# A causal convolution moved whole onto TensorE, in eight phases, two channel tiles side by side

## The chip, the cores and the metric

The program runs on one core of a Trainium2 chip. The metric is device time in microseconds (us) of one launch; the kernel before takes 1869.24 us, the median of three runs (1868.62 to 1869.81).

## The reference, cut to what matters

The whole model is two blocks (mixer, cross attention, MLP, then a conformer convolution, feed-forward, banded attention, feed-forward) on 512 tokens of width 1024 in float32. The change is in the convolution alone:

```python
def conformer_conv(x, w_pw1, b_pw1, w_dw, b_dw, ln_g, ln_b, w_pw2, b_pw2):
    a = jax.nn.glu(x @ w_pw1 + b_pw1, axis=-1)          # 1024 -> 2 x 1024, gated
    y = lax.conv_general_dilated(a, w_dw[:, None, :], window_strides=(1,),
        padding=((CONV_WIDTH - 1, 0),), feature_group_count=D_MODEL) + b_dw   # 31 taps, each channel for itself
    y = jax.nn.silu(layernorm(y, ln_g, ln_b))           # mean and variance over the 1024 channels of a token
    return y @ w_pw2 + b_pw2
```

Each channel has its own 31 taps over the last 31 tokens. LayerNorm needs all 1024 channels of a token before the first product with w_pw2.

## The kernel before, in words

Activations lie with channels on the 128 partitions: eight tiles t = 0 to 7 of 128 channels, 512 tokens along the free axis. A product in float32 precision is made of three fp32r matmuls (high by high, low by high, high by low, lines 396 to 398), so one output tile of a 1024-wide product takes 24 matmuls of 512 columns. Weights come by DMA as units of 512 KB (`raw`, on the queue of SyncE), and ScalarE and VectorE split each into `wH` and `wL`.

The convolution stage, `ph_con`, goes over the tiles: for tile t TensorE makes the value half `pa` and the gate half `pg`; `open_gates(t - 1)` makes the gated tile on VectorE and ScalarE. Then the taps. Two tiles (DIRECT) are done on VectorE: `chains` is a generator of 31 multiply-adds per tile, and `fill(n)` slips n of them between other work. Six tiles (PHASED) go to TensorE: the gated tile is written with its tokens sorted by token number modulo 4, and `to_phases` sends it to DRAM (`ph0x` to `ph7x`) and reads it back so that a partition is (phase, 32 channels). A convolution is then nine matmuls with small weight matrices for each group of 32 channels, whose output has tokens on the partitions; `phased(t)` makes 4 groups x 9 matrices. The matrices come from DRAM in loads of 16 (1 MB, tile `mat`, on the queue of GpSimd) into the pool `a8` of eight buffers; four of these hold the input x until the last pointwise matmul has read it, so that four or eight loads can be there at a time. A load waits until the matmuls have read the load whose buffer it takes.

A float32 matmul appears in the trace as two records, one for each half of the weights; an fp32r matmul and a transpose appear as one.

`take(t)` adds the bias and puts the result into `Y` (tokens on partitions, channels along the free axis), `bn_stats` makes sums over it, and after the last tile `bn_aggr` joins them, `newton` makes the reciprocal root, `normalise` applies it on `Y`, `turn` transposes back on TensorE, and `gate` applies SiLU and splits the result for the product with w_pw2. `keep_warm` (line 473) issues matmuls of no use while TensorE would wait.

The stage lies within `tc.manual_schedule()`: what order the code is written in is the order on each engine; DMAs of the SyncE queue are issued in their order, and each issue waits for what it needs before the next can go. The taps of the last tile (`phased(last, ...)`) stand behind those of tiles 5 and 6 and the transposes of the DIRECT tiles. In the chain and timeline rows `pc` is the bank that taps write, `xp` a tile read back in phases, `mat` the weight matrices, `glu` a gated tile, `ct` the transposes, `cz` and `ycH` the SiLU and its high part. In the banded attention, later in the program, `bo` is the product of weights with values: line 1771 writes it by halves of 64 columns of the array, j = 0 and 1 in turn.

Of the kernel before, what the change touches and what calls it, by code (L numbers as in the profile page):

```python
# [53 lines left out]


DIRECT, PHASED = [0, 1], [2, 3, 4, 5, 6, 7]

CHAIN = (6, 6, 6, 10, 10, 10, 10, 8)

NMAT = 9  # L60
# [7 lines left out]
WARM = (13, 22, 5)  # L68
# [28 lines left out]
def shape_constants():  # L97
# [8 lines left out]
    for h in range(8):  # L106
# [5 lines left out]
    return np.concatenate([ident, ones, causal, glam, reset, sel, oh, neg], axis=1)  # L112
# [3 lines left out]
      "reset": (512, 512), "sel": (1024, 8), "oh": (1032, 384), "neg": (1416, 384)}  # L116
# [113 lines left out]
def matrix_order():  # L230

    return [(t, g, m) for t in PHASED for g in range(4) for m in range(NMAT)]


def pack_matrices(inp):


    w = np.asarray(inp["conv_w_dw_2"])[0]
    order = matrix_order()
    out = np.zeros((-(-len(order) // 16), P, 16, P), np.float32)  # L240
    for n, key in enumerate(order):
        a = out[n // 16, :, n % 16, :]
        t, g, m = key
        c = np.arange(32)
        for s in range(4):
            for r in range(4):
                k = 4 * m + s - r - 2
                if 0 <= k < TAPS:
                    a[32 * s + c, 32 * r + c] = w[k, t * P + 32 * g + c]
    return out  # L250
# [21 lines left out]
class Builder:  # L272
# [1116 lines left out]
    def ph_con(self, ph):  # L1389
        nc, tc = self.nc, self.tc  # L1390
        x = self.x
        with tc.tile_pool(name="pc", bufs=1) as pool:

            Y = pool.tile([P, 4, D], F32, name="cY")
            bdw = pool.tile([P, D], F32, name="cb")
            stat = pool.tile([P, 4, (NT + 1) * 6], F32, name="cst6")
            nc.sync.dma_start(out=bdw, in_=bass.AP(self.row.tensor, self.row.offset, [[0, P], [1, D]]))
            wd = lambda t, k: self.col("w_dw", t * TAPS + k)
            gates, glus, xs, banks, mats, done = {}, {}, {}, {}, [], {}
            place = {key: n for n, key in enumerate(matrix_order())}  # L1400
            W_ = 4 * (P + NMAT - 1)
# [13 lines left out]
            def padded(name):  # L1415
                return pool.tile([P, W_], F32, tag="glu", name=self.nm(name), bufs=6)


            def to_phases(t):
                d = self.dp.tile([P, W_], F32, name=f"ph{t}x")  # L1420
                nc.sync.dma_start(out=d, in_=glus[t])
                xp = xs[t] = padded("xp").rearrange("p (g q) -> p g q", g=4)
                q = W_ // 4
                for s in range(4):
# [3 lines left out]
            def phased(t, gs=range(4)):  # L1428

                ps = banks[t] = self.bank("pc")  # L1430
                for g in gs:
# [5 lines left out]
            def chains():  # L1437
                for t in DIRECT:
                    while t not in glus:
                        yield  # L1440
                    acc = [pool.tile([P, S], F32, tag="cy", name=self.nm("cy"), bufs=3) for _ in range(2)]
                    for k in range(TAPS):
                        a, tap = acc[k % 2], glus[t][:, 2 + k:2 + k + S]
                        if k < 2:
                            nc.vector.tensor_scalar(a, tap, wd(t, k), None, ALU.mult)
                        else:
                            nc.vector.scalar_tensor_tensor(a, tap, wd(t, k), a, ALU.mult, ALU.add)
                        yield
# [369 lines left out]
```

## Time and profile before

| what | us |
|---|---|
| median of three runs | 1869.24 |
| the profiled execution, its own time | 1869.69 |
| its span in the trace | 1867.9 |
| TensorE busy (9177 matmul records) | 1845.1 (99%) |
| weight loads of TensorE, beside matmuls | 1515.9 (81%) |
| VectorE busy | 974.4 (52%) |
| ScalarE busy | 692.8 (37%) |
| GpSimd busy | 240.5 (13%) |
| DMA queue of SyncE, share of 16 engines | 27.8% |
| DMA queue of GpSimd, share of 16 engines | 3.6% |

The chain of work that ended last lies on TensorE for 88% of the span, and the granted clock of TensorE is 0.997 over the span. The taps on TensorE (line 1433) are 3% of that chain. Times in the rows below are microseconds from the start of the span.

### The profile page before, as it was taken

The page shows a single profiled execution, that of the slowest core. Times are in us where ns is not written, and L with a number is a line of the kernel's source. Part 1 is how long each engine was busy: PE and PEld are TensorE (multiplying, and loading weights), DVE is VectorE, ACT ScalarE, POOL GpSimd, SP SyncE. Part 2 cuts the span into 40 slices and gives each one's busy share as a digit, 9 for nine tenths or more (in the row PEclk, how much of TensorE's full clock was granted, in tenths as well). Part 3 has the DMA queues.
Part 4 walks back from the last instruction along what each step waited for, and adds up shares of the span by engine and source line. Part 5 has one row for each costly group of instructions (what it writes and reads, how often), then busy time and mean ns, then how long its engine had stood idle before and what let it go on. Part 6 is the DMA issues. An engine that isn't in the chain of part 4 may idle for free.

```text
span 1867.9 us, 23231 instructions
## 1 busy us (share of the span) xinstructions
PE 1845.1 (99%) x9177; PEld 1515.9 (81%) x9177; DVE 974.4 (52%) x1690; ACT 692.8 (37%) x1136; POOL 240.5 (13%) x237
## 2 busy tenths in 40 slices
PE   9999999999999999999999999999999999999997
PEld 6877778888888888889788888888877888888886
DVE  6658755765343444586654434245677444343444
ACT  5546654543232324311233223133566432132232
POOL 0111001020000000200022001011354211010110
PEclk9999999999999999999999999999999999999998
DMA  5313222122332323456132332654221232323321
GB/s 188 104 58 128 87 90 91 58 90 92 101 100 92 101 91 101 168 172 223 62 113 97 103 102 84 119 146 138 91 68 35 79 95 97 101 88 96 101 90 55
DMA packets 60653, 191.32 MB, mean 102 GB/s; under 512 B 6352, under 2 KB 16592, under 8 KB 58752
## 3 DMA queue, kind: packets, MB, share of 16 engines
q1 hardware_dynamic: 55152, 169.04, 27.8%
q0 software_dynamic: 2720, 17.83, 3.6%
q10 hardware_dynamic: 2672, 2.97, 0.5%
q8 instruction: 72, 1.18, 0.3%
q14 instruction: 37, 0.30, 0.1%
HBM read 182.90 MB, written 6.91 MB: 102 GB/s over the span
## 4 chain that ended last, share of the span: by engine, by line
PE 88%; issue 4%; DVE 4%; ACT 2%; DMA 1%; POOL 1%; SPq 0%; POOLq 0%; ACTq 0%; DVEq 0%
PE mm L396 26%; PE mm L397 26%; PE mm L398 26%; PE pc L1433 3%; DMA raw<-in_w_dram 1%; DVE wL L375 1%; PE bo L1771 1%; DVE q L1679 1%; PE fs L880 1%; PE ft L895 1%; PE fo L908 1%; ACT wH L374 1%; PE ps L506 0%; PE bs L1728 0%; PE bt L1754 0%
## 5 line engine op out<-in xcount | busy, mean ns | idle before, releaser
L374 ACT CAST wH<-raw 128x1024 fp32r<-128x1024 f32 (+1 forms) x304 | 315.5, 1041 | 881.6 <-PE mm L397 623.2
L396 PE MATMUL mm<-xH,wH 128*128 128x512 f32 x1232 | 481.5, 391 | 0.9 <-ACT wH L356 0.6
L397 PE MATMUL mm<-xL,wH 128*128 128x512 f32 x1232 | 479.7, 389 | 1.0 <-DVE xL L537 1.0
L398 PE MATMUL mm<-xH,wL 128*128 128x512 f32 x1232 | 479.6, 389 | 0.0
L375 DVE TENSOR_TENSOR wL<-raw,wH 128x1024 fp32r<-128x1024 f32 (+1 forms) x304 | 371.3, 1222 | 114.6 <-ACT wH L374 106.0
L396 PEld LDWEIGHTS mm<-xH,wH 128*128 128x128 f32 x1232 | 231.3, 188 | 50.8 <-issue 1.7
L397 PEld LDWEIGHTS mm<-xL,wH 128*128 128x128 f32 x1232 | 231.3, 188 | 48.7 <-DVE xL L537 1.3
L398 PEld LDWEIGHTS mm<-xH,wL 128*128 128x128 f32 x1232 | 231.3, 188 | 48.3 <-DVE wL L357 0.2
L396 PE MATMUL mm<-hidH,wH 128*128 128x512 f32 (+1 forms) x615 | 237.9, 387 | 0.0
L397 PE MATMUL mm<-hidL,wH 128*128 128x512 f32 (+1 forms) x615 | 237.8, 387 | 0.0
L398 PE MATMUL mm<-hidH,wL 128*128 128x512 f32 (+1 forms) x615 | 237.7, 387 | 0.0
L550 DVE TENSOR_TENSOR h<-mm,h 128x512 f32<-128x512 f32 x103 | 71.1, 691 | 263.7 <-PE mm L398 263.7
L499 POOL TENSOR_TENSOR ssq<-ssq,sq 128x512 f32<-128x512 f32 (+1 forms) x49 | 78.3, 1598 | 626.3 <-ACT sq L498 619.6
L1372 POOL TENSOR_TENSOR g<-g,rbc 128x512 f32<-128x512 f32 x44 | 75.1, 1708 | 538.3 <-ACT g L1371 538.3
L396 PEld LDWEIGHTS mm<-hidH,wH 128*128 128x128 f32 x615 | 115.5, 188 | 24.1 <-issue 0.6
L397 PEld LDWEIGHTS mm<-hidL,wH 128*128 128x128 f32 x615 | 115.5, 188 | 23.4
L398 PEld LDWEIGHTS mm<-hidH,wL 128*128 128x128 f32 x615 | 115.5, 188 | 23.4
L1373 DVE TENSOR_TENSOR g<-mm,g 128x512 f32<-128x512 f32 x44 | 30.1, 691 | 124.0 <-PE mm L398 119.4
L1370 DVE TENSOR_TENSOR g<-mm,rbc 128x512 f32<-128x512 f32 x44 | 30.2, 691 | 100.5 <-PE mm L398 98.5
L1339 DVE SCALAR_TENSOR_TENSOR u<-mm,rbc 128x512 f32<-128x512 f32 x32 | 21.9, 691 | 76.9 <-PE mm L398 75.8
L396 PE MATMUL mm<-wH,xH 128*128 128x512 f32 (+1 forms) x160 | 60.2, 376 | 0.0
L398 PE MATMUL mm<-wH,xL 128*128 128x512 f32 (+1 forms) x160 | 59.0, 369 | 0.0
(326 smaller groups left out, 2344.1 us busy)
## 6 DMA issues: line engine op xcount, KB each, us to landing
raw<-in_w_dram SPq DMA_DIRECT2D x272, 512.0 KB, 3.5
mat<-in_mat_dram POOLq DMA_DIRECT2D x14, 1024.0 KB, 7.5
raw<-in_w_dram SPq DMA_DIRECT2D x32, 448.0 KB, 3.2
rel<-rt POOLq DMA_DIRECT2D x1, 3072.0 KB, 35.6
h<-in_x_dram SPq DMA_DIRECT2D x8, 256.0 KB, 5.3
raw<-in_w_dram SPq DMA_DIRECT2D x8, 256.0 KB, 5.5
bias<-rel SPq DMA_DIRECT2D x1, 2048.0 KB, 8.9
mem<-in_mem_dram ACTq DMA_DIRECT2D x4, 256.0 KB, 3.7
```

The costliest lines, as they stand in the source:

```text
L374: self.nc.scalar.copy(H[:, :n], raw[:, :n])
L375: self.low = lambda: self.nc.vector.tensor_tensor(L[:, :n], raw[:, :n], H[:, :n].bitcast(F32), ALU.subtract)
L396: mm(out, lhsT=aH, rhs=bH, start=start, stop=False)
L397: mm(out, lhsT=aH, rhs=bL, start=False, stop=False)
L398: mm(out, lhsT=aL, rhs=bH, start=False, stop=stop)
L499: (eng or nc.gpsimd).tensor_tensor(self.ssq[:, :n], self.ssq[:, :n], q[:, :n], ALU.add)
L550: nc.vector.tensor_tensor(self.h[:, t, :], ps, self.h[:, t, :], ALU.add)
L1339: nc.vector.scalar_tensor_tensor(t, ps, 0.0, rb, ALU.max, ALU.mult)
L1370: nc.vector.tensor_tensor(g, pg, rb, ALU.mult)
L1372: nc.gpsimd.tensor_tensor(g, g, rb, ALU.mult)
L1373: nc.vector.tensor_tensor(g, pu, g, ALU.mult)
L1433: nc.tensor.matmul(ps[:, g * P:(g + 1) * P], lhsT=xs[t][:, g, m:m + P], rhs=matrix(t, g, m), start=m == 0, stop=m == NMAT - 1)
```

## The change

All eight tiles go through TensorE, so DIRECT, PHASED, CHAIN, `chains`, `fill` and `turned` are gone. Tokens are sorted modulo 8 (RP), channels in groups of 16 (GC), and five matrices (NMAT) do for the 31 taps. The stationary operand of a tap is now 128 partitions x 64 columns (NQ), and tile 2i writes output partitions 0 to 63 while tile 2i+1 writes 64 to 127 of the same bank, their matmuls in turn. A pair of tiles takes 2 x 8 groups x 5 matrices = 80 matmuls; four pairs take 320, with 20 loads of matrices instead of 14. Pair 0 is put behind the pointwise matmuls of tile 4, pair 1 behind those of tile 6, pair 2 and pair 3 behind those of tile 7.

A tile is read back from DRAM by eight DMAs instead of four. `Y` holds, on each partition, half of a token's channels, so the statistics of a token lie on two partitions: the `bn_stats` sets are summed by VectorE, and two small matmuls with the constant `both` add the two partitions, first for the mean, then for the variance.

```diff
-DIRECT, PHASED = [0, 1], [2, 3, 4, 5, 6, 7]
-CHAIN = (6, 6, 6, 10, 10, 10, 10, 8)
-NMAT = 9
+RP, GC, NQ = 8, 16, 64
+NMAT = 5
-WARM = (13, 22, 5)
+WARM = (13, 10, 7, 3, 12)
...
-                return pool.tile([P, W_], F32, tag="glu", name=self.nm(name), bufs=6)
+                return pool.tile([P, W_], F32, tag="glu", name=self.nm(name), bufs=8)
...
-                for s in range(4):
-                    nc.sync.dma_start(out=xp[32 * s:32 * s + 32],
-                                      in_=bass.AP(d.tensor, d.offset + s * q, [[W_, 32], [32 * W_, 4], [1, q]]))
+                for s in range(RP):
+                    nc.sync.dma_start(out=xp[GC * s:GC * s + GC],
+                                      in_=bass.AP(d.tensor, d.offset + s * q_, [[W_, GC], [GC * W_, P // GC], [1, q_]]))
...
-                        nc.tensor.matmul(ps[:, g * P:(g + 1) * P], lhsT=xs[t][:, g, m:m + P], rhs=matrix(t, g, m),
-                                         start=m == 0, stop=m == NMAT - 1)
+                        for j in range(2):
+                            nc.tensor.matmul(ps[j * NQ:j * NQ + NQ, n * P:(n + 1) * P],
+                                             lhsT=xs[2 * i + j][:, g, m:m + NQ], rhs=matrix(2 * i + j, g, m),
+                                             start=m == 0, stop=m == NMAT - 1)
...
-                    open_gates(t - 1, CHAIN[t - 1])
-                    if t - 3 in PHASED:
-                        take(t - 3)
-                    if t - 2 in PHASED:
-                        phased(t - 2)
-                open_gates(last, CHAIN[last])
+                    open_gates(t - 1)
+                    if t in (4, 6):
+                        pair(t // 2 - 2)
+                    if t in (5, 7):
+                        taken(t // 2 - 2)
+                open_gates(last)
...
-                take(last - 2)
-                phased(last - 1)
-                for _ in chain:
-                    pass
+                pair(2)
                 W = [self.unit(ahead=0) for _ in range(4)]
-                for t in DIRECT:
-                    turned(t)
-
-                phased(last, range(3))
...
+                taps(3, halves[0])
+                taken(2)
+
+                taps(3, range(4, 7))
...
-                for r in range(4):
-                    nc.vector.bn_aggr(mv[:, r, :], stat[:, r, :])
...
+                nc.vector.reduce_sum(mr, sets[:, :, :, 1], axis=AX.X)
+                nc.tensor.matmul(ps4[1][:, :RP], lhsT=both, rhs=mr, start=True, stop=True)
+                self.keep_warm(ps4[0], WARM[3])
+                nc.vector.tensor_scalar(mean, ps4[1][:, :RP], 1.0 / (2 * n), None, ALU.mult)
+                nc.vector.tensor_tensor(dev, sets[:, :, :, 1], mean.unsqueeze(2).to_broadcast([P, RP, n]), ALU.subtract)
+                nc.vector.tensor_tensor(dev, dev, dev, ALU.mult)
+                nc.vector.scalar_tensor_tensor(dev, dev, D / (2.0 * n), sets[:, :, :, 2], ALU.mult, ALU.add)
+                nc.vector.reduce_sum(v, dev, axis=AX.X)
+                nc.tensor.matmul(ps4[2][:, :RP], lhsT=both, rhs=v, start=True, stop=True)
+                self.keep_warm(ps4[0], WARM[4])
```

On TensorE before, from the last pointwise matmul (`mm_7085`) through the taps of tiles 5 and 6 (`pc_7176`, `pc_7243`) to the transposes of a DIRECT tile:

```order
L397 MATMUL mm_7085<-xL_6084,wH_7018 128x512
L398 MATMUL mm_7085<-xH_6083,wL_7019 128x512
L1433 MATMUL pc_7176<-mat_7070,xp_7013 128x128 x4
L1433 MATMUL pc_7176<-mat_7181,xp_7013 128x128 x16
L1433 MATMUL pc_7176<-mat_7199,xp_7013 128x128 x16
L1433 MATMUL pc_7243<-mat_7244,xp_7146 128x128 x16
L1433 MATMUL pc_7243<-mat_7262,xp_7146 128x128 x16
L1433 MATMUL pc_7243<-mat_7280,xp_7146 128x128 x4
L1463 MATMUL pc_7298<-kst,cy_6524 128x128 x4
```

On TensorE now, from the last pointwise matmul (`mm_7145`) to pair 2 (tiles 4 and 5: `xp_6932`, `xp_7031`), and its end with the beginning of pair 3 (tiles 6 and 7: `xp_7204`, `xp_7253`):

```order
L396 MATMUL mm_7145<-xL_6084,wH_7040 128x512
L397 MATMUL mm_7145<-xH_6083,wL_7041 128x512
L1438 MATMUL pc_7264<-mat_7265,xp_6932 64x128
L1438 MATMUL pc_7264<-mat_7265,xp_7031 64x128
...
L1438 MATMUL pc_7311<-mat_7338,xp_6932 64x128
L1438 MATMUL pc_7311<-mat_7338,xp_7031 64x128
L1438 MATMUL pc_7362<-mat_7363,xp_7204 64x128
L1438 MATMUL pc_7362<-mat_7363,xp_7253 64x128
```

Between the last pointwise matmul and the first tap of tile 7 there stood 72 matmuls of 128 output partitions and 8 transposes; now 80 matmuls of 64 output partitions stand there, and the first matmul but one of pair 3 reads tile 7.

On the queue of SyncE before, around the last two tiles (`raw` is a weight unit):

```order
L1421 DMA ph6x<-glu_7141 128x544
L1425 DMA xp_7146<-ph6x 32x4x136 x4
L339 DMA raw_7157<-in_w_dram 128x1024
L339 DMA raw_7165<-in_w_dram 128x1024
L1421 DMA ph7x<-glu_7224 128x544
L1425 DMA xp_7229<-ph7x 32x4x136 x4
```

The same place now:

```order
L1425 DMA ph6x<-glu_7199 128x544
L1428 DMA xp_7204<-ph6x 16x8x68 x8
L338 DMA raw_7217<-in_w_dram 128x1024
L338 DMA raw_7223<-in_w_dram 128x1024
L1425 DMA ph7x<-glu_7248 128x544
L1428 DMA xp_7253<-ph7x 16x8x68 x8
```

The order is the same; each tile has eight reads behind its write instead of four, in pieces of 68 elements instead of 136.

On VectorE before, from the last `take` to the first steps of `newton` (`s` are small columns, `cst` the sets of the statistics):

```order
L1472 TENSOR_TENSOR cY<-pc_7358,cb 128x4x32
L1483 BN_STATS cst_6353<-cY 128x6 x4
L1551 BN_AGGR s_7401<-cst_6353 128x2 x4
L1553 TENSOR_SCALAR s_7406<-s_7401 128x4
L482 TENSOR_SCALAR s_7410<-s_7406 128x4
```

On VectorE now (`mm_7493` and `mm_7494` are the banks of the two small matmuls on TensorE):

```order
L1448 TENSOR_TENSOR cY<-pc_7471,cb 128x8x16
L1453 BN_STATS cst_6353<-cY 128x6 x8
L1525 TENSOR_REDUCE s_7510<-cst_6353 128x8
L1528 TENSOR_SCALAR s_7507<-mm_7493 128x8
L1529 TENSOR_TENSOR dev_7506<-cst_6353,s_7507 128x128
L1530 TENSOR_TENSOR dev_7506<-dev_7506 128x128
L1531 SCALAR_TENSOR_TENSOR dev_7506<-dev_7506,cst_6353 128x128
L1532 TENSOR_REDUCE s_7508<-dev_7506 128x8
L1535 TENSOR_SCALAR s_7508<-mm_7494 128x8
L481 TENSOR_SCALAR s_7535<-s_7508 128x8
```

Eight `bn_stats` instead of four stand behind the last `take`, the four aggregates are gone, and seven instructions with two trips to TensorE stand before `newton`.

## Rows read from the trace of the kernel before

**Rows 1.** Stretch, length, busy us of PE PEld DVE ACT POOL, PEclk, DMA, GB/s.

```profile
823.60:905.60 82.00, 82.00 (x586) 76.25 (x586) 57.02 (x106) 11.91 (x14) 5.28 (x10) 1.00 0.62 214
```

**Rows 2.** Chain of work, taps and transposes: start us, us, what.

```profile
823.80 8.04 PE pc L1433 x72
...
880.66 16.08 PE pc L1433 x144
896.74 0.96 PE pc L1463 x8
897.69 8.04 PE pc L1433 x72
```

**Rows 3.** Timeline of TensorE, banded attention: start us, us, engine, line, what, count.

```profile
1368.34 0.44 PE L1771 MATMUL bo<-bpt,vv 128*64 128x128 f32 x4 [1.37 <-ACT bpt L1756]
1368.71 0.50 PE L396 MATMUL mm<-xqH,wH 128*128 128x512 f32 x1
...
1370.67 0.60 PE L1754 MATMUL bt<-kst,bs 128*128 128x128 f32 x4
1371.20 0.66 PE L1771 MATMUL bo<-bpt,vv 128*64 128x128 f32 x8
1371.79 0.50 PE L396 MATMUL mm<-xqH,wH 128*128 128x512 f32 x1
```

**Rows 4.** Timeline of GpSimd: loads of tap matrices, idle time before.

```profile
827.67 0.53 POOL L1407 DMA_DIRECT2D mat<-in_mat_dram  x1 [54.69 <-PE pc L1433]
...
878.01 1.05 POOL L1407 DMA_DIRECT2D mat<-in_mat_dram  x2 [10.12 <-PE mm L398]
880.73 1.05 POOL L1407 DMA_DIRECT2D mat<-in_mat_dram  x2 [1.67 <-PE mm L398]
```

**Rows 5.** DMA issues: count, KB each, median us from issue to landing.

```profile
mat<-in_mat_dram POOLq DMA_DIRECT2D x1, 1024.0 KB, 6.1
ph4x<-glu SPq DMA_DIRECT2D x1, 272.0 KB, 6.0
...
ph2x<-glu SPq DMA_DIRECT2D x1, 272.0 KB, 2.0
...
xp<-ph7x SPq DMA_DIRECT2D x4, 68.0 KB, 2.1
```

**Rows 6.** Timeline of the SyncE queue, last two tiles.

```profile
871.05 3.07 SPq L1425 DMA_DIRECT2D xp<-ph6x  x4
...
884.44 0.33 SPq L1421 DMA_DIRECT2D ph7x<-glu  x1
893.17 1.76 SPq L1425 DMA_DIRECT2D xp<-ph7x  x4
```

**Rows 7.** Timeline of VectorE, gate of tile 7.

```profile
881.90 1.41 DVE L1447 SCALAR_TENSOR_TENSOR cy<-glu,cst,cy 128x512 f32<-128x512 f32 x2
...
883.26 1.15 DVE L1500 SCALAR_TENSOR_TENSOR glu<-ca,cst,cg 128x512 f32<-128x512 f32 x1
```

**Rows 8.** Timeline of VectorE, statistics and normalisation.

```profile
906.10 0.47 DVE L1483 BATCH_NORM_STATS2 cst<-cY 128x6 f32<-128x32 f32 x4
906.49 1.15 DVE L1551 BATCH_NORM_AGGREGATE s<-cst 128x2 f32<-128x54 f32 x4
...
910.14 1.88 DVE L1566 TENSOR_SCALAR cY<-cY,s,s 128x128 f32<-128x128 f32 x7
```

**Rows 9.** Chain of work behind the last tap.

```profile
905.74 4.81 PE mm L473 x22
```

**Rows 10.** Timeline of TensorE near the end: one product at two clocks.

```profile
1855.68 0.70 PE L529 MATMUL ps<-dg,kst 128*128 128x256 f32 x2
1858.70 1.22 PE L529 MATMUL ps<-dg,kst 128*128 128x256 f32 x2 [2.32 <-DVE dg L524]
```

**Rows 11.** Busy time as in rows 1: first matmuls of the program; the end.

```profile
0.92:4.28 3.36, 3.36 (x8) 1.16 (x9) 0.00 (x0) 1.49 (x2) 0.36 (x1) 1.00 0.69 177
1858.00:1860.00 2.00, 1.22 (x2) 0.50 (x2) 1.96 (x6) 0.00 (x0) 0.00 (x0) 0.50 0.00 0
```

More of the change, by code (lines that the diff above doesn't have):

```diff
@@ L230, in matrix_order @@
 def matrix_order():
[L232 removed]
+    return [(2 * i + j, g, m) for i in range(NT // 2) for g in range(P // GC) for m in range(NMAT) for j in range(2)]
 def pack_matrices(inp):
@@ L1428, in phased @@
-            def phased(t, gs=range(4)):
-                ps = banks[t] = self.bank("pc")
-                for g in gs:
-                    for m in range(NMAT):
-                        nc.tensor.matmul(ps[:, g * P:(g + 1) * P], lhsT=xs[t][:, g, m:m + P], rhs=matrix(t, g, m),
-                                         start=m == 0, stop=m == NMAT - 1)
-            def chains():
-                for t in DIRECT:
[L1439 to L1448, printed above, removed]
-                    nc.vector.tensor_tensor(acc[0], acc[0], acc[1], ALU.add)
-                    done[t] = acc[0]
-                    yield
@@ new lines, in take, with statistics @@
+            def take(i, gs):
+                ps = banks.pop((i, gs[0]))
+                n = len(gs)
+                cs = slice(gs[0] * GC, (gs[-1] + 1) * GC)
+                split = lambda v: v.rearrange("p r (g c) -> p r g c", c=GC)
+                nc.vector.tensor_tensor(split(Y[:, i, :, cs]), ps[:, :n * P].rearrange("p (g r c) -> p r g c", r=RP, c=GC),
+                                        split(bdw[:, i, cs].unsqueeze(1).to_broadcast([P, RP, n * GC])), ALU.add)
+            def statistics(i, b):
+                for r in range(RP):
+                    nc.vector.bn_stats(stat[:, r, 2 * i + b, :], Y[:, i, r, b * 64:b * 64 + 64])
@@ L1486, in open_gates, with pair, taken @@
+            halves = [range(4), range(4, 8)]
+            def pair(i):
+                for gs in halves:
+                    taps(i, gs)
+            def taken(i):
+                for b, gs in enumerate(halves):
+                    take(i, gs)
+                    statistics(i, b)
+            def open_gates(u):
                 pa, pg = gates.pop(u)
@@ L1545, in ph_con @@
-                phased(last, [3])
-                take(last, [3], 1)
+                taps(3, halves[0])
+                taken(2)
+                taps(3, range(4, 7))
+                take(3, halves[0])
+                statistics(3, 0)
+                taps(3, [7])
+                take(3, range(4, 7))
+                take(3, [7])
+                statistics(3, 1)
                 ps4 = [self.bank("mm") for _ in range(4)]
                 self.keep_warm(ps4[0], WARM[1])
-                mv = self.small([P, 4, 2])
@@ L1550, in ph_con @@
-                for r in range(4):
-                    nc.vector.bn_aggr(mv[:, r, :], stat[:, r, :])
-                v, R, mr = (self.small([P, 4]) for _ in range(3))
-                nc.vector.tensor_scalar(v, mv[:, :, 1], EPS, None, ALU.add)
-                self.newton(v, 4, R)
-                nc.vector.scalar_tensor_tensor(mr, mv[:, :, 0], -1.0, R, ALU.mult, ALU.mult)
+                sets = stat.rearrange("p r e (o f) -> p r (e o) f", f=3)
+                n = 2 * NT
+                dev = self.tmp([P, RP, n], name="dev")
@@ L1596, in ph_con @@
                     for c in range(1, 4) if t < 4 else ():
                         drain(self.fm_steps(ps4[c], W[c], yy, [t], 0, 7))
+                    if t + 2 < NT:
+                        gate(t + 2)
+                    if t % 2 == 0 and t + 4 < NT:
+                        normalise(t // 2 + 2)
             for t in range(NT):
```

147 lines of the change are left out of this document (59 added, 88 removed).

## The prediction, made before the changed kernel ran

> **What bounds the kernel now.** I read the share of busy time first, then busy time stretch by stretch, then the chain of waits with the timelines of the convolution stage. In the stretch of the taps TensorE is busy for all of its 82 us at a granted clock of 1.00, VectorE for 57 [rows 1], and the chain runs over TensorE from tap to tap [rows 2]. So the order of work on TensorE sets the time, and a microsecond taken out there is a microsecond won, if what TensorE needs next is already there. Two things are not there by much. Tile 7's gated data is sent to DRAM at 884.44, and the read-back starts only at 893.17, when that write has landed; the four reads take 1.76 us to issue and 2.1 us to land [rows 5, 6], so the last, issued near 894.5, is there at about 896.7, and TensorE begins tile 7 at 897.69 [rows 2]: one microsecond to spare. And the matrix loads wait for TensorE to let buffers go [rows 4].
>
> I call T the end of the last pointwise matmul, 880.66 [rows 2].
>
> **The taps.** Now they cost 3 x 8.04 + 16.08 + 0.96 + 8.04 = 49.2 us of TensorE (of the 8.04 pieces one more lies between those shown; 72 records are 36 matmuls, 0.11 us a record) [rows 2]. After, 320 matmuls, 640 records. What a record costs when two column halves take turns is shown by `bo`: four records need 1368.71 - 1368.34 = 0.37 us, eight 1371.79 - 1371.20 = 0.59, so four more cost 0.22, 0.055 each, half of a full-width record, and 0.15 is for getting out [rows 3]. Getting in: the four full-width records before `bo` need 0.53 instead of 0.44, another 0.1 [rows 3]. 640 x 0.055 = 35.2, and four blocks at 0.25 add 1.0. Change: -49.2 + 35.2 + 1.0 = **-13.0**. The lower bound is this; the upper is that long runs of pairs do not overlap (a rival below).
>
> **The 62 multiply-adds on VectorE**, two of them 1.41 us [rows 7], go. They lay beside TensorE and gain nothing of themselves, but two stand between the gate of tile 7 and its write. Without them the write is issued some 1.0 us earlier, at T + 2.8 instead of T + 3.8 (not 1.4, since the sigmoid of ScalarE is then waited for; between 0 and 1.4).
>
> **Matrix loads.** A pair takes 80 matrices, five loads, and four are there when pair 0 or pair 1 starts. The fifth needs the buffer of the first. Before, the issue came at 827.67, 3.87 us after the taps' start at 823.80, of which 32 records at 0.11 are 3.5 [rows 2, 4]; now 16 matrices are read in 1.76 us, so the issue comes at 2.3 with the entry, and a load alone takes 6.1 to land [rows 5]: 8.4 us after the start. TensorE wants it after 64 x 0.11 + 0.15 = 7.2. That is a wait of 1.2 us in each of pairs 0 and 1, **+2.4** (from 0, if a load comes faster, to +5, if weights or `ph4x` share the engines). Pair 2 waits less, since buffers of x come free at 878 and 880.7 [rows 4].
>
> **The wait at pair 3.** This is the large term. From T on, 16.08 + 0.96 = 17.0 us of work on TensorE lay between tile 7's pointwise matmuls and its taps [rows 2]. Now only pair 2 lies there, 8.8 + 0.25 = 9.1 us. Is tile 7 back by T + 9.1? Its write needed 8.7 us with four matrix loads issued between 878 and 881.8 under way, 6.0 with one, 2.0 with none [rows 4, 5]; after, the same four are issued at the same distance from T, and two more at about T + 2.5 and T + 4.3, when pair 2 has read its first loads. So the write lands near T + 2.8 + 8.7 = T + 11.5. Then eight reads: issue takes 1.76 / 4 = 0.44 each on quiet queues and 3.07 / 4 = 0.77 with a matrix load under way [rows 6]. Lower end: T + 11.5 + 8 x 0.44 + 2.0 = T + 17.0. Upper end: T + 11.5 + 8 x 0.77 + 4.0 (the reads then land late as well) = T + 21.7. I take T + 18.3, nearer to the quiet row, because the last matrix load is through by then. TensorE stands from T + 9.1 to T + 18.3: **+9.2** (ends: 7.9 and 12.6; and 1.0 if nothing is queued in front, see the rivals).
>
> The page "DMA: Bandwidth & Descriptors" of the Trainium skill, under "Specifications", wants transfers of at least 512 bytes for full rate and says that smaller ones are read, changed and written back. The pieces read back are 68 floats, 272 bytes, where they were 544, and no row here shows reads below 512. By the rule, if it doubled the 2.1 us in which the reads of tile 7 land, tile 7 would come 2.1 later and the sum below would be +6.4.
>
> **The clock.** TensorE has never stood so long in the convolution. Near the end of the program it stood 2.32 us, and the same product that took 0.70 took 1.22 after it, with the granted clock at 0.50, which is 1.2 GHz instead of 2.4 [rows 10, 11]. How long the slow level lasts once work is back is shown by the program's beginning: eight matmuls in 3.36 us, 0.42 each [rows 11], where the same warming matmuls take 4.81 / 22 = 0.22 later [rows 9]. So about 3.4 us go at half rate and 1.7 us are lost: **+1.7** (0 if the clock holds, 4.4 if pairs of half-width matmuls are half as good at getting it back).
>
> **The statistics.** From the last tap to the first normalised slice there are 910.14 - 905.74 = 4.4 us [rows 8, 9]. Out goes the aggregate, 1.15 [rows 8]. In come four more `bn_stats` on 64 columns (four on 32 took 0.47 [rows 8]; 0.6), seven instructions on 8 to 128 columns between 0.2 and 0.33 (a slice of 128 columns takes 1.88 / 7 = 0.27 [rows 8]; 2.0 in all), and two trips to TensorE and back. No row shows such a trip alone; from below it is nothing, from above 1 us each with the ten warming matmuls (2.2 us) that stand in front of the first. I take 1.1 for both. The first transposes then need eight slices of which VectorE makes six, not three: 0.8. Sum -1.15 + 0.6 + 2.0 + 1.1 + 0.8 = **+3.3** (1.5 to 5). The warming matmuls hide none of this: they fill the wait.
>
> **The product w_pw2.** Transposes come by eight in place of four, and the second group needs all eight slices behind the first split on VectorE. TensorE is late there by about 1 us, and waits a little less at the end: **+0.7** (-0.5 to 2), an estimate from the slices in rows 8.
>
> SyncE's queue has four more reads per tile (1.8 to 3.1 us of issue), which delay the weight units behind them; a unit is split about one tile (48 matmuls of 0.22 [rows 9]) before it is used, so I cost this at nothing; without that cover each late unit would cost TensorE what it is late. The eight `bn_stats` and two `take` per pair lie under the pointwise matmuls.
>
> **Sum:** -13.0 + 2.4 + 9.2 + 1.7 + 3.3 + 0.7 = +4.3 us, on the profiled execution's own 1869.7: 1874.0. That execution lies 0.45 above the median of the runs, so I forecast 1873.5.
>
> **Rivals.** First, the read-back is not behind the matrix loads: the write lands in 2.0 as `ph2x` did, the reads in 8 x 0.44 + 2.1, tile 7 is there at T + 10.1, the wait is 1.0 and the clock stays. -13.0 + 2.4 + 1.0 + 3.3 + 0.7 = -5.6, 1863.6. For it speaks only that `ph2x` met no load; against it four writes that met one (`ph4x` 6.0, `ph7x` 8.7) [rows 5, 6].
>
> Second, the queues share each DMA engine evenly: the write waits for a share of one load only, about 2.5 us of it, and lands after 4.5; tile 7 is there at T + 13.2 and the wait is 4.1. -13.0 + 2.4 + 4.1 + 1.7 + 3.3 + 0.7 = -0.8, 1868.4. `ph7x` with 8.7 speaks against it, `ph4x` less so.
>
> The page "DMA: Bandwidth & Descriptors" of the Trainium skill, under "Queues, rings and completion order", has an engine go round its queues packet by packet, which would be this second rival; the rows fit better with a write that lands after all loads issued before it.
>
> Third, slower: the half-width matmuls overlap in short runs like `bo`'s only, because in a long run the weight loads of both halves (PEld was busy 76 of 82 us [rows 1]) set the pace, and each record costs 0.11. Then 640 x 0.11 = 70.4; the waits go, since pair 2 lasts 17.6 us; -49.2 + 70.4 + 1.0 + 0.4 + 3.3 + 0.7 = +26.6, 1895.8. It decides from a record cost of 0.08 up.
>
> Fourth, the forecast with its upper ends (wait 12.6, clock 3.4): -13.0 + 2.4 + 12.6 + 3.4 + 3.3 + 0.7 = +9.4, 1878.6.
>
> **How the numbers follow.** No change, for this kernel, is within 0.2%, 3.7 us: 1865.5 to 1873.0. The forecast has 0.56, its own range 1870 to 1877; its middle lies just over the line, so I give 0.36 of it to slower and 0.20 to no change. First rival 0.12, all faster. Second 0.18, no change. Third 0.04 and fourth 0.10, both slower. Faster 0.12, same 0.38, slower 0.50. The range from 1864.5 to 1880 leaves out the first rival's middle and the third, 0.16.
>
> **What would show it.** In the profile after, `pc` records in pairs every 0.11 us; one wait of about 1 us inside pairs 0 and 1 put down to `mat`; then on TensorE, behind pair 2, a gap of about 9 us before pair 3 that ends with `xp<-ph7x`, and a granted clock of 0.5 for some microseconds behind it; and about 7 us instead of 4.4 from the last tap to the first normalised slice. A gap under 3 us would make the forecast wrong, and a pace of 0.11 us a record too.

## The result and the profile after

The changed kernel takes 1881.7 us (median of four runs, 1881.5 to 1883.1) against 1868.9 before: ratio 1.0070, 95% interval 1.0052 to 1.0087. It is slower by 12.8 us; 1873.5 was forecast and the range ended at 1880. A second set of runs gave 1882.5 against 1869.7.

TensorE of the changed kernel, taps in the order pair 0, pair 1, pair 2, pair 3 (start, length, instruction, what ended the idle time):

```profile
822.83 7.21 PE L1438 MATMUL pc<-mat,xp 128*64 128x128 f32 x128
833.73 3.68 PE L1438 MATMUL pc<-mat,xp 128*64 128x128 f32 x32 [3.70 <-DMA mat<-in_mat_dram]
...
860.10 7.21 PE L1438 MATMUL pc<-mat,xp 128*64 128x128 f32 x128
868.37 1.97 PE L1438 MATMUL pc<-mat,xp 128*64 128x128 f32 x32 [1.06 <-DMA mat<-in_mat_dram]
...
881.38 9.17 PE L1438 MATMUL pc<-mat,xp 128*64 128x128 f32 x162
902.80 11.10 PE L1438 MATMUL pc<-mat,xp 128*64 128x128 f32 x158 [12.25 <-DMA xp<-ph7x]
```

The same places in the kernel before, the first taps behind tile 4's pointwise matmuls and those behind the last pointwise matmul:

```profile
823.64 8.20 PE L1433 MATMUL pc<-mat,xp 128*128 128x128 f32 x72
880.50 16.24 PE L1433 MATMUL pc<-mat,xp 128*128 128x128 f32 x144
```

128 records take 7.21 us, 0.056 each: the pace is the forecast one [rows 3]. Where [rows 2] showed TensorE without a break it now waits three times: 3.70 and 1.06 us for the fifth matrix load of a pair, 12.25 for tile 7. T, the end of the last pointwise matmul, is 881.38 where the same timeline had 880.50 (the chain of [rows 2] puts it at 880.66). In the first wait and in the third the clock falls to the lower of its two levels: the 32 records behind the first take 3.68 us, 0.115 each, at a granted clock of 0.50. The stretch of these records, by windows (start and end, length, busy us of PE PEld DVE ACT POOL, PEclk, DMA share, GB/s):

```profile
833.70:837.30 3.60, 3.57 (x32) 3.28 (x32) 2.56 (x8) 0.97 (x1) 0.00 (x0) 0.50 0.98 416
```

The whole stretch by windows, in the same columns, kernel before:

```profile
823.00:860.00 37.00, 37.00 (x238) 33.35 (x237) 26.21 (x44) 5.21 (x6) 2.12 (x4) 1.00 0.64 221
860.00:880.00 20.00, 20.00 (x126) 17.94 (x125) 12.75 (x21) 2.60 (x3) 2.11 (x4) 1.00 0.62 193
880.00:892.00 12.00, 12.00 (x107) 11.88 (x107) 8.28 (x16) 4.09 (x5) 1.05 (x2) 1.00 0.91 360
892.00:903.00 11.00, 11.00 (x100) 11.00 (x99) 9.09 (x21) 0.00 (x0) 0.00 (x0) 1.00 0.43 126
```

and after:

```profile
823.00:860.00 37.00, 33.30 (x256) 28.62 (x254) 13.15 (x30) 5.43 (x6) 2.63 (x5) 0.91 0.73 240
860.00:881.00 21.00, 19.94 (x208) 17.60 (x208) 8.36 (x24) 2.83 (x3) 3.68 (x7) 1.00 0.95 335
881.00:893.00 12.00, 9.55 (x164) 8.95 (x163) 7.38 (x18) 4.19 (x5) 2.10 (x4) 1.00 1.03 416
893.00:901.50 8.50, 0.00 (x0) 0.00 (x0) 0.88 (x7) 0.00 (x0) 0.00 (x0) 0.54 0.89 301
```

The last two columns say more than the first five. Before, the DMA engines have room in all windows but one. After, from 860 on, they have none: shares of 0.95 and 1.03, 335 and 416 GB/s, and still 0.89 while TensorE does nothing at all. VectorE, which lost its multiply-adds, is idle for most of it.

What was issued between 880 and 903 after (count, KB each, median us from issue to landing):

```profile
mat<-in_mat_dram POOLq DMA_DIRECT2D x4, 1024.0 KB, 13.8
raw<-in_w_dram SPq DMA_DIRECT2D x3, 512.0 KB, 4.3
ph7x<-glu SPq DMA_DIRECT2D x1, 272.0 KB, 9.0
xp<-ph7x SPq DMA_DIRECT2D x8, 34.0 KB, 7.2
```

The matrix load of [rows 5] that took 6.1 was a lone one. The four issued around T, when the buffers of x come free, took 10.0 us in the kernel before (median; 878.0 to 881.3) and 10.9 now (878.8 to 882.1), and tile 7's write took 8.7 and 9.0: so far little is new. New are the two loads that pair 2 sets free behind them, at 883.66 and 885.40:

```profile
mat<-in_mat_dram POOLq DMA_DIRECT2D x2, 1024.0 KB, 15.2
```

They landed at 898.0 and 901.4, and tile 7's reads, 2.1 us before, took 7.2. The queue of SyncE shows the eight reads issued without a pause, in 0.46 us each (in [rows 6] 0.44), so it is their landing that is late, not their issue:

```profile
884.16 0.33 SPq L1425 DMA_DIRECT2D ph7x<-glu  x1
893.19 3.66 SPq L1428 DMA_DIRECT2D xp<-ph7x  x8
```

In the 4 us from 893 to 897 the queue of the loads (q0) had nearly all of the DMA engines' time and that of SyncE (q1) next to none (packets, MB, share):

```profile
q0 software_dynamic: 232, 1.65, 99.5%
q1 hardware_dynamic: 17, 0.00, 0.5%
```

Behind the taps, TensorE with the two trips of the statistics (L1526, L1533), the transposes and the first product of `w_pw2`:

```profile
913.83 2.36 PE L472 MATMUL mm<-warm 128*128 128x512 bf16 x10
916.02 0.28 PE L1526 MATMUL mm<-s,cbo 128*128 128x8 f32 x2
...
917.93 0.39 PE L1533 MATMUL mm<-s,cbo 128*128 128x8 f32 x2 [0.96 <-DVE s L1532]
...
921.34 1.63 PE L1553 MATMUL ct<-kst,cY 128*128 128x128 f32 x8 [0.38 <-DVE cY L1548]
...
924.28 0.50 PE L395 MATMUL mm<-ycH,wH 128*128 128x512 f32 x1
```

and the same product before:

```profile
913.15 0.58 PE L396 MATMUL mm<-ycH,wH 128*128 128x512 f32 x1
```

From the end of the last tap (913.89) to that product it is 10.39 us, against 7.41 before (905.74 in [rows 9] to 913.15).

### The profile page after: what moved, and what is told of

It is laid out like the page before. It is cut to its first block, busy times and chain, and to the rows that moved or that the text cites. A ratio compares the mean times of both kernels' runs of the same rounds, so it can differ in the third digit from the quotient of the medians.

```text
span 1880.1 us, 23726 instructions
## 1 busy us (share of the span) xinstructions
PE 1839.6 (98%) x9386; PEld 1508.0 (80%) x9386; DVE 941.0 (50%) x1667; ACT 696.0 (37%) x1145; POOL 242.9 (13%) x243
## 4 chain that ended last, share of the span: by engine, by line
PE 81%; issue 8%; DVE 4%; DMA 3%; ACT 2%; POOL 1%; SPq 0%; POOLq 0%; ACTq 0%; DVEq 0%
PE mm L395 25%; PE mm L396 25%; PE mm L397 24%; DVE wL L374 1%; DMA mat<-in_mat_dram 1%; DMA raw<-in_w_dram 1%; PE pc L1438 1%; ACT wH L373 1%; PE bo L1756 1%; DVE q L1664 1%; PE fs L879 1%; PE ft L894 1%; PE fo L907 1%; DMA ph7x<-glu 0%; PE bs L1713 0%
```

## The experiments

Theory A: the DMA engines, loaded with 20 matrix loads, bring tile 7 and the fifth matrices late, and the idle time costs clock. Rival B: the eight small reads are slow of themselves. Rival C: the longer statistics are the loss. All edits are to the changed kernel, cut to the lines that matter.

**No matrix loads behind the fourth.** The taps of later tiles use the first four blocks again, so the output is not the convolution's.

```diff
-                load_matrices(n // 16 + 1 - len(mats))
-                return mats[n // 16][:, n % 16, :]
+                load_matrices(min(n // 16 + 1, 4) - len(mats))
+                return mats[n // 16 % 4][:, n % 16, :]
```

> Left out: every matrix load behind the fourth; the taps of later tiles use the first four blocks of matrices again, so the output is not the convolution's, while every matmul, write and read-back stays. Theory A (the 13 us won on the taps are given back because the fifth load of a pair, tile 7's write and its reads land behind matrix loads, and the clock falls in the waits): no wait inside pairs 0 and 1, tile 7's write lands about 2 us after its issue, its reads about 2 us after theirs, tile 7 is there near T + 10.5, the wait in front of pair 3 is 1 to 2 us, the clock stays at 1.00, and the time is 1859 to 1863 us. Rival B (the eight small reads and their issue on SyncE are what is late): the reads still land 6 us or more after their issue, the wait stays at 7 us or more, time 1870 or more. Rival C (the loss is the longer tail of the statistics): the tail does not change, so the time stays within 3 us of 1881.7.

1863.8 us (1861.0 to 1865.4), ratio to before 0.9969 (0.9956 to 0.9982). There is no wait in pairs 0 to 2, and tile 7's transfers are quick:

```profile
ph7x<-glu SPq DMA_DIRECT2D x1, 272.0 KB, 4.1
xp<-ph7x SPq DMA_DIRECT2D x8, 34.0 KB, 2.0
```

The reads land in 2.0 us, and the stretch from the last tap to `w_pw2` is 10.37 as in the changed kernel, while 18 us are gone: B and C fall. The time lies 0.8 above A's range, which was 1 to 2 us too hopeful: the write took 4.1 us, with nothing of this kernel's data in front of it (why stays open), tile 7 came at T + 12.1, the wait was 3.1 and the clock fell for 3.4 us.

**More work as cover.** Pair 1 behind tile 7's pointwise matmuls.

```diff
-                    if t in (4, 6):
-                        pair(t // 2 - 2)
-                    if t in (5, 7):
-                        taken(t // 2 - 2)
+                    if t == 4:
+                        pair(0)
+                    if t == 5:
+                        taken(0)
...
+                pair(1)
                 pair(2)
+                taken(1)
```

> Pair 1's taps are moved from behind tile 6's pointwise matmuls to behind tile 7's, in front of pair 2, so that 18 us of work on TensorE lie between tile 7's pointwise matmuls and its taps instead of 9. Theory A: tile 7 comes at T + 21 at the latest; of the 12.3 us wait some 9 are covered and the clock does not fall for it, but the matrix loads of pairs 1, 2 and 3 now crowd together, so up to 5 us of waits on matrices come instead: 1870 to 1876 us. Rival B expects the same cover and the same gain, without waits on matrices: about 1870. Rival C: no change from 1881.7.

1885.1 us (1883.2 to 1888.7): all three theories miss. T is 871.87. Between 870 and 903:

```profile
mat<-in_mat_dram POOLq DMA_DIRECT2D x10, 1024.0 KB, 16.6
ph7x<-glu SPq DMA_DIRECT2D x1, 272.0 KB, 12.4
xp<-ph7x SPq DMA_DIRECT2D x8, 34.0 KB, 16.8
```

and TensorE's waits in the taps:

```profile
PE pc L1438 <- DMA xp<-ph7x: 12.9, 1, 12.9
PE pc L1438 <- DMA mat<-in_mat_dram: 7.6, 5, 4.1
```

Twice the cover and nearly the same wait, 12.9 for 12.25: the pairs that were to cover it also release buffers, and each release sends another megabyte. How tile 7 lands among them shows in the issues, taken one by one (when issued, when landed):

| matrix loads | reads of tile 7 |
|---|---|
| 877.64, 894.8 | 887.09, 895.3 |
| 879.39, 897.8 | 887.46, 898.3 |
| 881.13, 900.7 | 887.94, 901.2 |
| 882.88, 903.7 | 888.40, 904.3 |
| 885.99, 907.4 | 888.88, 907.4 |

The two queues take turns, and a turn of the loads is a whole megabyte, some 3 us: each read lands behind one load, and the last three of the eight only when no load is left (907.6 to 908.0). So A is sharpened: not the distance to T counts but how many loads are under way together with tile 7's transfers.

**Reads of tile 7 from two engines.**

```diff
-                    nc.sync.dma_start(out=xp[GC * s:GC * s + GC],
+                    (nc.scalar if t == NT - 1 and s % 2 else nc.sync).dma_start(
+                                      out=xp[GC * s:GC * s + GC],
```

> Tile 7's eight reads are issued by two engines, four on SyncE and four on ScalarE. Theory A (the reads land behind the matrix loads): tile 7 is complete when the last matrix load has landed, within 1 us of where it is now (902.7 us from the span's start), the wait in front of pair 3 stays at 11 to 12.5 us and the time within 2 us of 1881.7. Rival B (the chain of eight issues, 0.43 us each, is what is late): the last read is issued 1.7 us earlier and lands as much earlier or more, the wait falls to 10.5 us or less, and the time to 1879.5 or less.

1879.9 us (1878.4 to 1881.8). All reads were issued by 894.6 instead of 896.4 and landed at 901.3 instead of 902.7, 1.5 us behind the last matrix load (899.8; 901.4 in the changed kernel):

```profile
xp<-ph7x SPq DMA_DIRECT2D x4, 34.0 KB, 6.8
xp<-ph7x ACTq DMA_DIRECT2D x4, 34.0 KB, 6.9
```

The wait of 10.7 lies between the two expectations, and the run does not decide: the issue came 1.8 us earlier, the last load 1.6 and the landing 1.4.

**The last three loads behind tile 7's reads.**

```diff
-                        nc.gpsimd.dma_start(out=m, in_=self.mat[len(mats)])
+                        (nc.sync if len(mats) > 16 else nc.gpsimd).dma_start(out=m, in_=self.mat[len(mats)])
...
+                load_matrices(17 - len(mats))
                 open_gates(last)
+                load_matrices(3)
```

> The last three matrix loads of pair 3 are issued by SyncE behind tile 7's eight reads instead of by GpSimd in front of them; nothing else changes, and as many bytes are moved. Theory A (small transfers land behind the matrix loads issued before them): tile 7's write has three matrix loads in front, lands near T + 9, the reads land 2 us after their issue, tile 7 is there near T + 14 instead of T + 21, the wait in front of pair 3 falls from 12.3 to about 5 us, two waits of about 1 us for matrices come inside pair 3, and the time is 1873 to 1877 us. Rival B (the eight small reads are late of themselves): the reads take 6 us or more as now, and with loads of the same bytes the end of pair 3 does not come earlier: 1880 or more.

1877.5 us (1875.5 to 1878.9). The wait for tile 7 fell to 8.4 us, less than expected since the write, with three loads in front, still took 9.0; the reads landed quickly:

```profile
mat<-in_mat_dram SPq DMA_DIRECT2D x3, 1024.0 KB, 6.9
ph7x<-glu SPq DMA_DIRECT2D x1, 272.0 KB, 9.0
xp<-ph7x SPq DMA_DIRECT2D x8, 34.0 KB, 2.0
```

As many bytes were moved, and the same pieces of 272 bytes landed in 2.0 instead of 7.2: B is out. (Three loads changed their queue as well as their place; but with all loads left to GpSimd the reads of the second warm run below, issued when no load was left, landed in 2.0 too.) Of the two short waits expected inside pair 3 none came. But the last matrices landed at 908.7 and the taps ended at 911.1, 2.8 us earlier than in the changed kernel (913.9): sorting a full queue wins little.

**Keeping the clock.** Fifty warming matmuls in front of pair 3.

```diff
                 W = [self.unit(ahead=0) for _ in range(4)]
+                self.keep_warm(self.bank("kw"), 50)
                 taps(3, halves[0])
```

> Fifty warming matmuls of 128 x 512 (0.22 us each, 11 us) are put on TensorE between pair 2 and pair 3, in the wait for tile 7. If the clock's fall is a term of its own: the wait stays 11 to 13 us with the warming matmuls in it, the granted clock stays 1.00 through pair 3, pair 3's first records take 0.055 instead of 0.113 us, and the time falls by 2 to 2.5 us against the changed kernel, to about 1879.3. If the clock costs nothing here (the taps then only start into another wait): no change, 1881.5 to 1882.

1881.7 us (1876.2 to 1883.1). The granted clock was 1.00 through pair 3, which took 8.92 instead of 11.09 us, yet the time stood; in this trace T was 1.5 us and tile 7 1.7 us later than in the changed kernel. Again, in five rounds beside the changed kernel:

> The kernel with the fifty warming matmuls in front of pair 3 once more, beside the changed kernel on one chip, since 0.2 us could not be told in three rounds: in e4_warm the stretch from the start of pair 3 to the first product of w_pw2 was 2.1 us shorter than in the changed kernel, and T came 1.5 us later. If the clock's fall is a loss by itself: 1.5 to 2.5 us below the changed kernel in this call. If what it wins is lost elsewhere every time: within 0.7 us of it.

> The changed kernel once more, on the chip of the other two runs: 1880.5 to 1883 us. Theory A expects pair 0's length to be one of two values over the runs of this code, near 10 us where the fifth matrix load is issued before the second weight load, near 14.5 where it is issued after it; here it is 10 to 15.

1882.3 (1880.5 to 1885.8) against 1882.5 (1878.0 to 1884.4): no difference. What the clock alone is worth stays open, since in the trace of the second warm run it was not held: the warming matmuls ended 8 us before tile 7 came, and pair 3 took 10.84 us. That trace shows something else. Pair 0 had next to no wait (below), T came at 875.45, six us early; then

```profile
875.45 8.95 PE L1438 MATMUL pc<-mat,xp 128*64 128x128 f32 x160
884.33 11.11 PE L472 MATMUL kw<-warm 128*128 128x512 bf16 x49
...
903.87 1.55 PE L1438 MATMUL pc<-mat,xp 128*64 128x128 f32 x12 [8.06 <-DMA xp<-ph7x]
```

and the write of tile 7, issued at 878.72, took

```profile
ph7x<-glu SPq DMA_DIRECT2D x1, 272.0 KB, 19.0
xp<-ph7x SPq DMA_DIRECT2D x8, 34.0 KB, 2.0
```

In front of it on SyncE's queue lay reads of tile 6, of which the last five landed about one to a load, from 879.5 to 892.3, and two weight units. Tile 7 came at 903.7. TensorE ran ahead by 6 us, and the queue took it all back.

**SyncE's queue relieved for all tiles.** As the third experiment, for every tile.

```diff
-                    nc.sync.dma_start(out=xp[GC * s:GC * s + GC],
+                    (nc.scalar if s % 2 else nc.sync).dma_start(out=xp[GC * s:GC * s + GC],
```

> The reads of every tile are issued half by SyncE and half by ScalarE, so that SyncE's queue is 1.7 us shorter per tile. Theory A: the weight loads that stood just in front of pair 0's fifth matrix load are issued about 2 us earlier and are out of its way; it lands within 6.5 us of its issue, the waits inside pairs 0 and 1 fall to 1.5 us or less each without a fall of the clock there, tile 7 still comes behind the last matrix load (wait 10 to 12.5 us), and the time is 1876 to 1879. Rival B: the wait in front of pair 3 falls by 1.7 us or more too, 1875 or less. If ScalarE's queue is held up by the writes it now waits for, the evacuations come late and the time is 1882 or more.

1882.6 us (1880.2 to 1884.2). Pairs 0 and 1 took 9.3 and 9.4 us without a wait to speak of, as expected, and T was 875.1. But the way was another: the weight units were not issued earlier but later, at 826.89 and 828.03, behind the matrix load of 825.71. And the last branch of the expectation came true beside the delay of the run before: ScalarE, whose queue now held reads that waited for tile 6's write, stood for 16 us,

```profile
876.90 2.00 ACT L373 CAST wH<-raw 128x1024 fp32r<-128x1024 f32 x2 [15.96 <-issue]
```

tile 7's gate was opened at 883.7 and its write issued at T + 11.8, not T + 2.8; the write then took 11.2 us and the taps ended at 913.1.

**Why pair 0 sometimes waits.** In the changed kernel the second weight unit and the fifth matrix load were issued at 825.07 and 825.11, and landed after

```profile
mat<-in_mat_dram POOLq DMA_DIRECT2D x1, 1024.0 KB, 8.6
raw<-in_w_dram SPq DMA_DIRECT2D x1, 512.0 KB, 8.5
```

In the second warm run, the same code up to there, that unit was issued at 826.97, behind the matrix load of 825.69, which then took 5.1. Over the eight traces that load these matrices the rule holds without exception: pair 0 takes 9.3 to 9.7 us where the load comes first (four) and 14.6 to 15.5 where the unit does (four). Pair 1 agrees: its fifth load took 9.6 and 8.8 us in the two traces where a unit went out 0.3 and 0.6 us in front of it, and 5.2 to 6.0 in the five others that have it there. In the changed kernel 40 ns decided where the time was lost, but not whether: in its second trace the load went first and pair 0 took 9.6 us, pair 1 waited 4.66, and from the start of pair 0 to T it was 58.5 us in both. For the end it counts next to nothing:

| run | T | tile 7 complete | taps end | first w_pw2 product |
|---|---|---|---|---|
| changed kernel | 881.4 | 902.7 | 913.9 | 924.3 |
| reads from two engines | 881.7 | 901.3 | 912.5 | 922.8 |
| kept warm | 882.9 | 904.4 | 913.4 | 923.9 |
| kept warm, again | 875.5 | 903.7 | 914.7 | 925.2 |
| all reads from two engines | 875.1 | 902.2 | 913.1 | 923.4 |
| changed kernel, again | 883.2 | 904.9 | 916.4 | 926.7 |

T varies by 8 us, tile 7 by 3.6, and not together.

**Building the matrices.** A matrix is 8 x 8 blocks, each of them a diagonal of 16, so on each partition a load of 16 matrices is one product of 128 coefficients with a mask of 16 columns. First all twenty blocks are built, on VectorE and GpSimd (`k` is the block, `coef` holds the coefficients, `eye` the mask):

```diff
-                        nc.gpsimd.dma_start(out=m, in_=self.mat[len(mats)])
+                        (nc.gpsimd if k in ONPOOL else nc.vector).tensor_tensor(
+                            m.rearrange("p n (r c) -> p (n r) c", c=GC),
+                            coef[:, 16 * k:16 * k + 16, :].rearrange("p n r -> p (n r)").unsqueeze(2).to_broadcast([P, P, GC]),
+                            eye.unsqueeze(1).to_broadcast([P, P, GC]), ALU.mult)
```

then with fewer on GpSimd and pair 2's in front of pair 1's statistics, beside tile 7's reads from two engines as above:

```diff
-ONPOOL = (2, 5, 6, 7, 10, 11, 14, 16)
+ONPOOL = (2, 5, 6, 7)
...
+                    if t == 7:
+                        load_matrices(4)
+                        taken(1)
```

> The matrices are not loaded but built on the chip: 2560 coefficients per partition are loaded once (1.3 MB for 21), and each block of 16 matrices is one product of coefficients and a mask of 16 columns, 128 x 2048, twelve of them on VectorE and eight on GpSimd. VectorE had 46 us more of work in the kernel before than in the changed one; twelve products at 2.2 to 2.8 us (0.55 to 0.69 us per 512 columns) are 26 to 34 us, eight on GpSimd at 6.4 us are 51. Theory A: with the loads gone, the write and the reads of tile 7 land as they do alone, the wait in front of pair 3 is 1 to 3 us, the clock holds, and the time is 1859 to 1866 us, which would be faster than both kernels. Rival B: the reads stay late, 1870 or more. Rival C: within 3 us of 1881.7.

> As e5_build, with the matrices of pairs 2 and 3 all built on VectorE (in e5_build one block took 5.3 us on VectorE while GpSimd built another, and 2.28 alone), those of pair 2 in front of pair 1's statistics, and tile 7's eight reads issued by SyncE and ScalarE, four each. Theory A: pair 2 no longer waits for a matrix (it waited 3.31 us), tile 7's data is gated 1.4 us earlier, tile 7 is there near T + 9, pair 3 waits less than 1.5 us (4.21 before), the clock stays at 1.00 through the taps, and the time is 1859 to 1864 us, faster than both kernels. If building on VectorE delays the gates instead, pair 3's wait stays at 3 us or more and the time at 1868 or more.

1871.3 (1865.6 to 1874.2) and 1868.4 us (1866.2 to 1869.7; ratio to before 0.9994, 0.9985 to 1.0003): A's times were missed in both. Yet without loads tile 7's write landed in 2.1 us in both and its reads in 1.9 and in 2.2 to 2.4, so B does not stand either. Both move the wait to VectorE. In the first, pair 2 waited 3.3 us for a matrix and tile 7's gate opened at 883.0, 8.6 us behind T; in the second VectorE worked from 855.6 to 890 with hardly a pause and opened tile 7's gate at 877.2, 3.7 us behind T:

```profile
877.22 0.68 DVE L1480 TENSOR_TENSOR cg<-mm,rbc 128x512 f32<-128x512 f32 x1
```

**Loading fourteen, building six.** From these and the held-back loads: blocks 4, 9 and 15 to 17 on VectorE, 14 on GpSimd, 18 and 19 loaded by SyncE behind tile 7's reads, the rest as in the changed kernel; reads of tile 7 from two engines.

```diff
+BUILT, ONPOOL, ONSYNC = (4, 9, 14, 15, 16, 17, 18, 19), (14,), (18, 19)
...
+                load_matrices(15 - len(mats))
                 open_gates(last)
+                load_matrices(5)
```

> Twelve blocks of matrices are loaded by GpSimd as before (0 to 3, 5 to 8, 10 to 13), the fifth of pairs 0 and 1 and three of pair 3 are built on VectorE (2.28 us each), one on GpSimd, and the last two of pair 3 are loaded by SyncE behind tile 7's reads; those reads are issued by SyncE and ScalarE, four each. Theory A in its sharper form (in the stretch from pair 1 on the DMA engines move all they can, and what is issued late lands last): with 6 of the 10 last megabytes built, tile 7's write lands 2 to 3 us after its issue and its reads 2.5 us after theirs, tile 7 is there near T + 9.5, pairs 0, 1 and 2 wait less than 0.5 us each and pair 3 less than 1.5, the clock holds through the taps, the taps end near 893 us and the time is 1859 to 1863 us. If VectorE is the next bound (as in e7_built2, where it worked without a break from 855 to 890 and the gate of tile 7 began 3.5 us late): the wait before pair 3 is 3 us or more and the time 1865 or more.

1861.8 us (1861.4 to 1865.4), ratio to before 0.9961 (0.9949 to 0.9974): faster than both kernels, by 8 and by 20 us, and within the range expected. TensorE:

```profile
823.12 8.96 PE L1457 MATMUL pc<-mat,xp 128*64 128x128 f32 x160
...
873.97 9.16 PE L1457 MATMUL pc<-mat,xp 128*64 128x128 f32 x162
884.82 8.95 PE L1457 MATMUL pc<-mat,xp 128*64 128x128 f32 x158 [1.68 <-DMA xp<-ph7x]
```

One wait of 1.68 is left, a little more than expected since tile 7's write took 3.7 us; the clock stays at 1.00, the taps end at 893.8.

## Why the prediction was wrong

Its steps in the order of its sum, each by one trace of the changed kernel and one of the run with fourteen loads, which has the new taps without the waits:

| term | forecast | measured | from |
|---|---|---|---|
| taps | -13.0 | -13.1 | start to T and T to end of taps, without the 1.68: 50.9 + 18.1, before 56.9 + 25.2 |
| waits in pairs 0 and 1 | +2.4 | +7.7 | start to T: 58.55 against 50.85 |
| wait at pair 3 | +9.2 | +12.25 | the row of 902.80 |
| clock in pair 3 | +1.7 | +2.15 | T to end of taps 32.5, less 18.1 and 12.25 |
| statistics | +3.3 | +3.0 | 10.39 less 7.41 |
| w_pw2 | +0.7 | +1.1 | first product to end: 955.83, before 954.77 |
| start of pair 0 | 0 | -0.8 | 822.83, before 823.64 (824.67 in the second trace) |
| sum | +4.3 | +12.3 | spans: +12.2 |

The pace, the kind and place of each wait, the fall of the clock behind pair 3 and the tail were right. (For the clock the prediction read 3.4 us at half rate out of the program's first matmuls, but their row in [rows 11] shows a granted clock of 1.00: only their pace speaks for it. The size came out near, 2.15 for 1.7.) The step that failed is the matrix loads, and it failed in two places.

In pairs 0 and 1 the fifth load was priced as "a load alone takes 6.1 to land". That held in pair 1 (issued 862.37, it took 5.9; the wait was 1.06). In pair 0 the load went out beside a weight unit and took 8.6: the wait was 3.70 instead of 1.2, and the clock fell there too, for which the sum had nothing. Of the 7.7 us of the row the two waits are 4.8, which the term's upper end of 5 allowed; the other 2.9 are, for the most part, records at the lower clock.

At pair 3 the last load was taken to be "through by then". The two loads that pair 2 sends were issued where the prediction said, at T + 2.3 and T + 4.0, but landed at T + 16.6 and T + 20.0, and tile 7's reads with them: tile 7 came at T + 21.3 instead of T + 18.3, near the upper end of T + 21.7.

Both have one cause, which the prediction had no term for: no load was alone. In 823 to 903 the kernel moves

```profile
DMA packets 9479, 23.88 MB, mean 299 GB/s; under 512 B 5789, under 2 KB 5789, under 8 KB 7424
```

where before it moved

```profile
DMA packets 5689, 17.74 MB, mean 222 GB/s; under 512 B 640, under 2 KB 2688, under 8 KB 4402
```

[rows 1] had the number that was needed: a DMA share of 0.62 over 82 us leaves 31 us free. The taps are 13 us shorter, and six loads take 16 us of the DMA engines by an estimate from the changed kernel's trace (its sixteen loads in 823 to 903 take 54% of these 80 us, 2.7 each). So 2 us are left free of 69, which is nothing once the loads come bunched, and eleven of the sixteen were issued from 862 on. From 860 until tile 7 is there at 902.7 the kernel moves 14.9 MB; at the 416 GB/s of 881 to 893 that is 35.8 us by estimate, while TensorE wants tile 7 after 30.5 (at 890.55, when pair 2 is done). The prediction never made that sum. With it, the wait inside pairs and the wait at pair 3 are one cost and not two, which is why the runs that removed the first got the second back.

Two smaller steps fell with it. SyncE's longer queue was costed at nothing. Before, the two weight units in front of pair 0's fifth load were issued from 820.66 on, 7.0 us ahead of it; now from 824.59 on, 0.5 us ahead. Of the 3.9 us by which they come later, two are the longer queue (tile 3's reads take 3.81 us of issue instead of 1.75), and where a unit goes out just in front of a fifth load, that load is late. And the write was placed by its distance to T. T + 11.5 held in both traces of the changed kernel (T + 11.7 and T + 11.4), where the four loads around T lie in front of it as they did before; but in the second warm run, with T six us earlier, it landed at T + 22.3.

The first rival falls with the reads' 7.2 us. The run without the loads comes to its 1863.6 (1863.8), but by other parts: nothing in pairs 0 and 1 instead of 2.4, 3.1 at pair 3 instead of 1.0, and a clock that falls. The second, queues sharing evenly, falls too: the write took 9.0, not 4.5, and for 4 us the queue of the loads had 99.5% of the DMA engines' time. "DMA: Bandwidth & Descriptors" of the Trainium skill, under "Queues, rings and completion order", has an engine go round its queues packet by packet; the run with pair 1 behind tile 7 shows turns indeed, but each as long as a load of 1 MB. What the prediction held against it, that a write lands behind all loads issued before it, is not so either: the write issued at 884.16 landed at 893.1, ahead of two loads issued before it (882.05, landed 895.3, and 883.66, landed 898.0); in the kernel before, too, it landed at 893.2 and the last load in front of it at 893.8. The third, no overlap, falls with 0.056 us a record. The fourth, the upper ends (1878.6), came nearest; it left pairs 0 and 1 at 2.4, and with the upper end of that term too, 5, it would have been 1881.2. Terms that have one cause reach their upper ends together.

A doubling by the rule on 512 bytes in "DMA: Bandwidth & Descriptors" of the Trainium skill ("Specifications") is not seen: 34 KB in pieces of 272 bytes landed in 2.0 us where the queue was empty, 68 KB in pieces of 544 in 2.1 [rows 5]. No run compares transfers of one size, so the rate is not tested.

## What to carry to other kernels

When a change makes an engine faster, sum the bytes that will be moved up to each point where it needs data, and divide by what the DMA engines move when full; over a longer stretch the sum can fit and the bunched part of it not. A wait priced from a lone transfer is only a lower bound. Cover does not help if the covering work itself releases buffers and so starts transfers that take turns with the one that is waited for. What has structure can be cheaper to build on an engine that stands idle, but only as much of it as that engine has room for.

## What was not expected

- Small transfers wait for large ones of another queue: 34 KB took 1.9 to 2.0 us with nothing in front, 7.2 with three loads of 1 MB on the way, 16.8 with seven, most of the reads then landing one behind each load. There, more reads were more turns.
- The DMA engines moved 416 GB/s over 12 us on one core, all but 0.3 MB of it from DRAM into SBUF. "DMA: Bandwidth & Descriptors" of the Trainium skill ("Where 436 GB/s comes from") lets the memory side bind at about 358; the trace is nearer the other figure there, 435.
- VectorE builds a block of 128 x 2048 in 2.28 us alone, GpSimd in 3.7 at the least. At the same time they took 5.3 and 4.7, in the run that built all twenty on both:

```profile
872.40 10.64 DVE L1418 TENSOR_TENSOR mat<-cco,ceye 128x2048 f32<-128x2048 f32 x2
```

against four in 8.89 us in the next run, on VectorE alone. Together they built no more in that time than VectorE by itself.
